# Two heads' values in seven block products among other groups; x's block differences and one gate group at other places

## The chip, the cores and the metric

The kernel runs on one core of a Trainium2 chip, in one launch. The metric is the device time of that launch in microseconds. TensorE multiplies matrices, VectorE and ScalarE work on elements, GpSimd builds constants, SyncE (SP) issues nearly all loads. In rows of the profile they are PE (its weight loads PEld), DVE, ACT, POOL and SP.

## The reference

One decoder block on x of 256 tokens and 2048 columns, in float32:

```
h = rmsnorm(x)
q, k, v, g, gk, gb, gc, xc, ma, mb = split(h @ w_in)           # 16,400 columns
log_g = log_sigmoid(gk @ w_gk_up + b) / 16                     # 4 heads, key width 256, value width 512
o = rmsnorm(gated linear attention of q, k, v, log_g)          # in chunks of 64, per head
y_a = o * silu(g);  y_b = gb * conv3(gc * xc)                  # causal, depthwise
x = x + (sigmoid(ma) * y_a + sigmoid(mb) * y_b) @ w_out
out = rmsnorm(x + (silu(h2 @ w_gate) * (h2 @ w_up)) @ w_down)  # h2 = rmsnorm(x), 5632 wide
```

## The kernel before

Every matrix is streamed once from HBM in *pieces* of 128 x 1024 numbers (0.5 MB): four blocks of 128 rows of a 256-column group (k and q), or two of a 512-column group (all else). A piece is split on the chip: ScalarE casts it to `hi` (`high`, L238), VectorE subtracts to get `lo` (`low`, L243), and `mm3` (L347 to L349) makes each product out of three matmuls, so that float32 precision is kept. The buffers are 5 raw pieces, 6 `hi` and 5 `lo`. `stream_list` gives the order of all pieces; `take` keeps loads, casts and subtractions up to LOOK = 5 pieces ahead of TensorE. After each piece `used` counts a *tick*, and work registered with `later(delay, fn)` or `at(tick, fn)` is issued at its tick. The program is then scheduled per engine: an instruction that is ready in the scheduler's plan can pass an earlier one that isn't, except those under `pin`.

A 512-column group normally takes 8 pieces (`eights`): 2 blocks of rows x 2 halves of the tokens x 3 matmuls of 512 columns, 12 per piece. A *pair* of groups can be done with seven block products in place of eight (`sevens`): 28 steps of 6 matmuls. In each of four quarters q a step `11` uses a block of the first group, `t1`, `t3`, `t2` and `t4` use sums of blocks that VectorE forms first (`sum_of`, L259 and L265, from loads `y` and `x`), and at the end eight steps `21` and `22` use plain blocks again. `sevens` needs five PSUM banks and block differences of the tokens' side (`xsums`, formed by `x_blocks` at the ticks of X_AT, four quarters; `sum_blocks` makes four subtractions, a cast and a low half). Steps stand between plain pieces of other groups (`mixed`), since a step needs as much from VectorE as a plain piece or more.

The stages: `mm_first` does k0, q0, v0 together (16 pieces, ticks 0 to 16) while x, its norm, the decay tables and GpSimd's differences are made. Then for heads 1 to 3: k, q and v, each plain (`mm_cols`, `mm_tok`); `scale_rows` scales k and q, `decayed` multiplies them into the decay tables, `scores` makes the scores, `values` splits v into `vh` and `vl`, `attend` multiplies (9 matmuls, `o_ps`), `head_norm` scales with the head's norm. Then the gates, in the order of GATES: g0 plain, and four pairs gc/xc in seven products with plain ma, gb, mb and g groups between, and gb3, mb3. At the third piece of g0 the heads' memory (`gla`, `gpool`) is given back, and the pools of the gates take its place, among them the one for `y` and `x`. A gate's result is merged (`merge`, `transpose_block`) while the next pair runs. Then come w_out, the feed-forward stage (its own pairs fg/fu among down pieces), and the last norm.

PSUM: banks b0 to b4 are for groups of five, b5, ax0 and ax1 are `lent` in turn to plain groups and transposes.

Of the kernel before, what the change touches and what calls it, by code (L numbers as in the profile page):

```python
# [8 lines left out]
F32 = mybir.dt.float32  # L9
# [11 lines left out]
H = 4  # L21
# [22 lines left out]
def plan():  # L44
# [61 lines left out]

def mixed(pair, eights, early=False):

    if pair is None:
        return eights  # L110
    sevens = seven_list(pair)
    sums = ("t1", "t3", "t2", "t4")
    gaps = [0] * len(sevens)
    rest = len(eights)
    while rest > 0:
        for some in (sums + ("11",) if early else sums, ("21", "22")):
            for n, (_, e) in enumerate(sevens):
                if e[0] in some and rest > 0:
                    gaps[n] += 1
                    rest -= 1  # L120
    out, put = [], 0
    for e, n in zip(sevens, gaps):
        out += [e] + eights[put:put + n]
        put += n
    return out


def gates_list():
    return [e for pair, keys in GATES
            for e in mixed(pair, [(key, k) for key in keys for k in range(0, KC, 2)], keys[0] == "gb2")]  # L130

# [45 lines left out]
def stream_list():  # L177

    pieces = [(p[0], p[3]) for p in piece_list()]
    out = [e for e in pieces if e[0][0] in "kqv"] + gates_list() + [e for e in pieces if e[0] == "wo0"]  # L180
    return out + hidden_list() + down_list()
# [3 lines left out]
def block_kernel(ctx, tc, x, xt, cols_in, gkw_in, gku_in, gnw, conv_w, finw, w_in, w_out, w_gu, w_dn, out):  # L185
# [25 lines left out]

    lent = ["b5", "ax0", "ax1"]


# [180 lines left out]

    count["sevens"] = 0

    def sevens(name, pool, a, s, second, done):

        r = 2 * count["sevens"]
        count["sevens"] += 1
        pa, pb, pc, pd, pe = (bank([P, 512], f"{name}_{i}", f"b{(r + i) % 5}") for i in range(5))
        v2, v3 = (pool.tile([P, 512], F32, tag=n, name=n) for n in ("v2", "v3"))
        u = {}
        for _ in range(28):
            piece, (what, q) = yield
            first, last = q == 0, q == 3
            if what == "11":  # L410
                quad(pa, lambda j: a(0, 4 * q + j), piece, first, last)
                if last:
                    nc.scalar.copy(v2, pa)
            elif what == "t1":
                quad(pb, lambda j: s(0, q, j), piece, first, last)
            elif what == "t3":
                quad(pd, lambda j: s(2, q, j), piece, first, last)
            elif what == "t2":
                quad(pc, lambda j: s(1, q, j), piece, first, last)
                if last:  # L420
                    u[1] = second(1)
                    nc.vector.tensor_tensor(out=v2, in0=pc, in1=v2, op=ALU.subtract)
                    nc.vector.tensor_tensor(out=v3, in0=pd, in1=v2, op=ALU.add)
# [12 lines left out]
        done(0, pa, u[0])  # L436
# [344 lines left out]
    at(25, tables_across)  # L781
    v_first = mm_first(gk_chunks, scale_rows)

# [3 lines left out]
    def x_blocks(q):  # L787
        pair = gpool.tile([P, NM, T], F32, tag="bc", name="xraw")
        raw, work = pair[:, 0:4, :], pair[:, 4:8, :].rearrange("p s (j c) -> p s j c", c=P)
        cs = slice(4 * q, 4 * q + 4)  # L790
# [3 lines left out]
    for q in range(4):  # L794
        at(X_AT[q], lambda q=q: x_blocks(q))


# [8 lines left out]
    def scores(i):  # L806

        ps = aux([P, 3, P], "sc_ps")
        ms = (2 * i, 2 * i + 1)
# [15 lines left out]

    o = [omain.tile([P, NT, DV], F32, tag=f"m{i}", name="o") for i in range(H)]
    sso = const.tile([P, NT, H], F32, name="sso")
    ro = const.tile([P, NT, H], F32, name="ro")

    def attend(i, vh, vl):  # L830
        sh, sl = sc.pop(i)
        ps = [aux([P, DV], "o_ps") for t in range(NT)]
        mm3(ps[0], sh[:, 0, :], sl[:, 0, :], vh[:, 0, :], vl[:, 0, :], True, True)
        mm3(ps[1], sh[:, 2, :], sl[:, 2, :], vh[:, 0, :], vl[:, 0, :], True, False)
        mm3(ps[1], sh[:, 1, :], sl[:, 1, :], vh[:, 1, :], vl[:, 1, :], False, True)
        for t in range(NT):
            nc.scalar.copy(o[i][:, t, :], ps[t])
            square_sum(o[i][:, t, :], sso[:, t, i:i + 1])

# [6 lines left out]
    split_v = {}  # L846
    for i in range(H):
        if i:
            for key, ps in [(key, mm_cols([key], xh, xl)[0]) for key in (f"k{i}", f"q{i}")]:
                scale_rows(key, ps)  # L850
        now = count["tick"]
        at(max(now + 1, 27 + i), lambda i=i: decayed(i, scaled_rows.pop(f"k{i}"), scaled_rows.pop(f"q{i}")))
        at(max(now + 3, 29 + i), lambda i=i: scores(i))
        vps = mm_tok(f"v{i}", KC, 512, xa) if i else v_first

        def values(i=i, vps=vps):
            vh = gpool.tile([P, NT, DV], F32R, tag="vh", name="vh")
            vl = gpool.tile([P, NT, DV], F32R, tag="vl", name="vl")
            for t in range(NT):
                nc.scalar.activation(vh[:, t, :], vps[t], AF.Copy, scale=r1[:, t:t + 1])  # L860
                nc.vector.scalar_tensor_tensor(out=vl[:, t, :], in0=vps[t], scalar=r1[:, t:t + 1],
                                               in1=vh[:, t, :].bitcast(F32), op0=ALU.mult, op1=ALU.subtract)
            split_v[i] = (vh, vl)

        if i:
            values()
        else:

            at(18, values)
        tick_of = max(count["tick"] + 1, 31)  # L870
        at(tick_of, lambda i=i: attend(i, *split_v.pop(i)))
        at(tick_of + 1, lambda i=i: head_norm(i))

# [93 lines left out]

    def begin_gate(key):
# [5 lines left out]
    xy = None  # L974
    steps = run(gates_list(), begin_gate)
    for n in steps:
        if n == 2:

# [155 lines left out]
    for _ in run(order, hidden):  # L1134
        pass
    count["gap"] = 1
    finb = sT.tile([P, D], F32, tag="sh", name="finb")
    nc.scalar.dma_start(finb, finw.to_broadcast([P, D]))
# [43 lines left out]
CONV_AT = 12  # L1182
X_AT = (50, 54, 58, 62)
H_AT = (2, 4, 6, 8)
# [56 lines left out]
```

## Time and profile before

| | |
|---|---|
| median of 3 runs | 1504.65 us (1503.75 to 1506.16) |
| the profiled execution | 1504.81 us, its span 1503.1 us |
| granted clock of TensorE, mean | 0.999 |
| matmuls | 7064 |
| read from HBM | 351.03 MB |

All numbers of a trace are those of the one profiled execution, and its times count from the start of the span. A timeline's row has start, duration, engine, line, operation, result <- operands, and in brackets the idle time before it with what ended it. Rows of TensorE overlap: a matmul of 512 columns shows 0.39 us, so the distance between starts tells the pace, not the duration. `lo`, `hi`, `y`, `x` and `o_ps` are the names in the program; all gc/xc matmuls carry the first name, `gc`.

### The profile page before, as it was taken

What the parts mean: (1) busy time and instruction counts of PE and PEld (TensorE: products, weight loads), DVE (VectorE), ACT (ScalarE), POOL (GpSimd) and SP (SyncE); (2) the same over time, 40 slices, a digit from 0 to 9 for tenths busy, and PEclk for the clock granted to TensorE, in tenths of its full rate; (3) what the DMA queues carried; (4) which work ended last, traced back from release to release, by engine and by line L of the source; (5) the groups of instructions that cost most, each with busy time, mean ns of one, the idle gap of its engine ahead of it and who ended that gap; (6) DMA issues with size and microseconds to landing.
All of it is one profiled execution on the core that took longest, in us unless ns stands there. A gap on an engine that the chain in (4) does not pass through costs nothing.

```text
span 1503.1 us, 19370 instructions
## 1 busy us (share of the span) xinstructions
PE 1489.7 (99%) x7064; PEld 1244.8 (83%) x7064; DVE 1277.8 (85%) x1283; ACT 864.1 (57%) x977; POOL 38.0 (3%) x60
## 2 busy tenths in 40 slices
PE   9999999999999999999999999999999999999997
PEld 8989988888887888888888888888888788888887
DVE  6785868979979878966689999999999999999975
ACT  7773546655655655654566755655565556565553
POOL 0030000000000000000000000000000000000000
PEclk9999999999999999999999999999999999999999
DMA  9656557876876878787677777776877788787782
GB/s 349 201 172 174 177 166 251 288 225 234 285 259 232 297 237 257 249 258 215 209 221 219 238 253 251 250 253 218 275 242 239 259 255 277 242 264 234 231 297 90
DMA packets 100128, 358.58 MB, mean 239 GB/s; under 512 B 11492, under 2 KB 11620, under 8 KB 99904
## 3 DMA queue, kind: packets, MB, share of 16 engines
q1 hardware_dynamic: 96656, 346.73, 70.8%
q0 software_dynamic: 2800, 8.89, 2.2%
q10 hardware_dynamic: 576, 1.72, 0.3%
q8 instruction: 55, 0.90, 0.2%
q14 instruction: 41, 0.34, 0.1%
HBM read 351.03 MB, written 2.10 MB: 235 GB/s over the span
## 4 chain that ended last, share of the span: by engine, by line
PE 53%; DVE 1%; issue 0%; ACT 0%; DVEq 0%; ACTq 0%
PE fg L347 8%; PE fg L349 8%; PE fg L348 8%; PE dn L347 5%; PE dn L349 5%; PE dn L348 5%; PE wo L347 2%; PE wo L348 2%; PE wo L349 2%; PE fu L349 1%; PE fu L347 1%; PE fu L348 1%; PE trb L595 1%; PE mb L349 0%; PE mb L348 0%
## 5 line engine op out<-in xcount | busy, mean ns | idle before, releaser
L243 DVE TENSOR_TENSOR lo<-raw,hi 128x1024 fp32r<-128x1024 f32 (+1 forms) x506 | 612.0, 1217 | 110.9 <-ACT hi L238 27.9
L238 ACT CAST hi<-raw 128x1024 fp32r<-128x1024 f32 (+1 forms) x506 | 523.9, 1047 | 269.9 <-PE gb L349 27.7
L238 ACT CAST hi<-x 128x1024 fp32r<-128x1024 f32 x144 | 151.7, 1053 | 267.4 <-DVE x L265 207.1
L243 DVE TENSOR_TENSOR lo<-x,hi 128x1024 fp32r<-128x1024 f32 x144 | 176.1, 1223 | 37.5 <-ACT hi L238 26.6
L347 PE MATMUL dn<-lo,acth 128*128 128x512 f32 (+1 forms) x368 | 140.7, 382 | 1.7 <-DVE h L1098 0.9
L349 PE MATMUL dn<-hi,acth 128*128 128x512 f32 (+1 forms) x368 | 139.9, 380 | 0.0
L348 PE MATMUL dn<-hi,actl 128*128 128x512 f32 (+1 forms) x368 | 139.9, 380 | 0.0
L265 DVE TENSOR_TENSOR x<-x,raw 128x1024 f32<-128x1024 f32 x96 | 117.0, 1218 | 12.0 <-DMA raw<-in_w_in_dram 7.7
L347 PE MATMUL fg<-lo,hh 128*128 128x512 f32 x288 | 112.4, 390 | 0.0
L349 PE MATMUL fg<-hi,hh 128*128 128x512 f32 x288 | 112.2, 390 | 0.0
L348 PE MATMUL fg<-hi,hl 128*128 128x512 f32 x288 | 112.2, 389 | 0.0
L347 PE MATMUL fg<-lo,sh 128*128 128x512 f32 x256 | 101.0, 395 | 0.0
L348 PE MATMUL fg<-hi,sl 128*128 128x512 f32 x256 | 99.9, 390 | 0.0
L349 PE MATMUL fg<-hi,sh 128*128 128x512 f32 x256 | 99.8, 390 | 0.0
L347 PEld LDWEIGHTS dn<-lo,acth 128*128 128x128 f32 x368 | 69.2, 188 | 15.8 <-DVE h L1098 1.8
L349 PEld LDWEIGHTS dn<-hi,acth 128*128 128x128 f32 x368 | 69.2, 188 | 13.3
L348 PEld LDWEIGHTS dn<-hi,actl 128*128 128x128 f32 x368 | 69.2, 188 | 12.9
L347 PEld LDWEIGHTS fg<-lo,hh 128*128 128x128 f32 x288 | 54.1, 188 | 11.8 <-DVE lo L243 0.5
L349 PEld LDWEIGHTS fg<-hi,hh 128*128 128x128 f32 x288 | 54.1, 188 | 11.3
L348 PEld LDWEIGHTS fg<-hi,hl 128*128 128x128 f32 x288 | 54.1, 188 | 11.0
L243 DVE TENSOR_TENSOR lo<-y,hi 128x1024 fp32r<-128x1024 f32 x48 | 58.5, 1218 | 4.8 <-ACT hi L238 2.1
L259 DVE TENSOR_TENSOR raw<-y,x 128x1024 f32<-128x1024 f32 x48 | 58.5, 1219 | 4.2 <-DMA y<-in_w_in_dram 3.3
(247 smaller groups left out, 3070.1 us busy)
## 6 DMA issues: line engine op xcount, KB each, us to landing
raw<-in_w_in_dram SPq DMA_DIRECT2D x254, 512.0 KB, 4.5
raw<-in_w_gu_dram SPq DMA_DIRECT2D x176, 512.0 KB, 4.4
raw<-in_w_dn_dram SPq DMA_DIRECT2D x88, 512.0 KB, 4.5
x<-in_w_gu_dram SPq DMA_DIRECT2D x32, 512.0 KB, 4.8
y<-in_w_gu_dram SPq DMA_DIRECT2D x32, 512.0 KB, 3.9
raw<-in_w_out_dram SPq DMA_DIRECT2D x32, 512.0 KB, 4.3
y<-in_w_in_dram SPq DMA_DIRECT2D x16, 512.0 KB, 4.4
x<-in_w_in_dram SPq DMA_DIRECT2D x16, 512.0 KB, 4.8
```

Of the source, the lines that this page charges most:

```text
L238: nc.scalar.copy(hi[:, ks, :], raw[:, ks, :])
L243: nc.vector.tensor_tensor(out=lo[:, ks, :], in0=raw[:, ks, :], in1=hi[:, ks, :].bitcast(F32), op=ALU.subtract)
L259: nc.vector.tensor_tensor(out=raw, in0=y, in1=held["x"], op=ALU.add)
L265: nc.vector.tensor_tensor(out=x, in0=x, in1=other, op=ALU.add)
L347: nc.tensor.matmul(ps, lhsT=sh, rhs=ml, start=first, stop=False, skip_group_check=onto)
L348: nc.tensor.matmul(ps, lhsT=sl, rhs=mh, start=False, stop=False, skip_group_check=onto)
L349: nc.tensor.matmul(ps, lhsT=sh, rhs=mh, start=False, stop=last, skip_group_check=onto)
L595: nc.tensor.transpose(out=ps[:, j, :], in_=src[:, j * P:(j + 1) * P], identity=ident)
```

## The change

Heads 2 and 3 no longer multiply v2 and v3 as two plain groups. They become the pair ("v2", "v3") of `sevens`. `heads_list` gives the new order: k1, q1 and half of v1 as before; then the pair's 28 steps, dealt among the rest of v1, k2, q2, k3, q3 and seven pieces of g0 (27 plain pieces); then four pieces of ma0, the last of g0, four of ma0. The heads' memory is given back after the fourth piece of ma0. The heads run in the same loop (`run`) as the gates now: `mm_cols` becomes `cols_group`, `values` of head 1 is registered at the end of its group, and `pair_values` splits heads 2 and 3 straight from the pair's banks. In GATES ma0 is gone, and g1, ma1, mb1, gb2 and others move one pair forward; the last pair has three plain groups beside it.

`x_blocks` moves from ticks 50, 54, 58 and 62 to 5, 8, 12 and 17, with its work in tiles of `omain`. Smaller edits: one buffer in place of two for `kr` and `qr` (head 1's scaling moves to tick 28), `attend` is issued per half of the tokens on lent banks, and squares are written in place.

```diff
 GATES = (
-    (None, ("g0",)),
-    (("gc0", "xc0"), ("ma0", "gb0", "mb0")),
-    (("gc1", "xc1"), ("g1", "ma1", "gb1")),
-    (("gc2", "xc2"), ("mb1", "g2", "ma2")),
-    (("gc3", "xc3"), ("gb2", "mb2", "g3", "ma3")),
+    (("gc0", "xc0"), ("g1", "gb0", "mb0")),
+    (("gc1", "xc1"), ("ma1", "gb1", "mb1")),
+    (("gc2", "xc2"), ("g2", "ma2", "gb2")),
+    (("gc3", "xc3"), ("mb2", "g3", "ma3")),
     (None, ("gb3", "mb3")),
...
+    def deal(some, most):
+        nonlocal rest
+        for n, (_, e) in enumerate(sevens):
+            if e[0] in some and most > 0 and rest > 0:
+                gaps[n] += 1
+                rest -= 1
+                most -= 1
+    if late is not None:
+        deal(("21", "22"), late)
+        while rest > 0:
+            deal(sums + ("11",), rest)
...
+def heads_list():
+    step = {"k": 4, "q": 4, "v": 2, "g": 2, "m": 2}
+    plain = [(key, k) for key in ("k1", "q1", "v1", "k2", "q2", "k3", "q3", "g0") for k in range(0, KC, step[key[0]])]
+    n = plain.index(("v1", 8))
+    gate = [("ma0", k) for k in range(0, KC, 2)]
+    return plain[:n] + mixed(("v2", "v3"), plain[n:-1], 4) + gate[:4] + plain[-1:] + gate[4:]
...
-                    u[1] = second(1)
+                    u[1] = pc if tags else second(1)
...
-        u[0] = second(0)
+        u[0] = pb if tags else second(0)
...
-        pair = gpool.tile([P, NM, T], F32, tag="bc", name="xraw")
+        raw, work = (omain.tile([P, 4, 2, P], F32, tag=tag, name=tag) for tag in ("m0", "m1"))
...
+    def pair_values(t, two, three):
+        if t == 1:
+            place_values(2)
+            both = gpool.tile([P, 2, NT, DV], F32R, tag="bc", name="both")
+            split_v[3] = [both[:, n] for n in range(2)]
+        for i, src in ((2, two), (3, three)):
+            split_value(i, t, src)
+        if t == 0:
+            for i in (2, 3):
+                later(i - 1, lambda i=i: attend(i, 0))
+                later(i - 1, lambda i=i: attend(i, 1, "b1"))
+                later(i, lambda i=i: head_norm(i))
...
+    def rows_done(key, ps):
+        i = int(key[1])
+        if i > 1:
+            scale_rows(key, ps)
+        else:
+            at(28, lambda: scale_rows(key, ps))
+        if key[0] == "q":
+            now = count["tick"]
+            at(max(now + 1, 28 + i), lambda: decayed(i, scaled_rows.pop(f"k{i}"), scaled_rows.pop(f"q{i}")))
+            at(max(now + 4, 31 + i), lambda: scores(i))
...
+    def begin_head(key):
+        if isinstance(key, tuple):
+            return sevens(key[0], held["pool"], xa, sums(xsums), None, pair_values, ("b4", "b0", "b2", "b1", "b3"))
+        if key[0] == "v":
+            return eights(key, xa, lambda ps: values(int(key[1]), ps))
+        tags = {"k1": ("b0", "b1"), "q1": ("b2", "b3")}.get(key)
+        return cols_group(key, xh, xl, rows_done, tags)
...
-        return eights(key, xa, gate(key), *([("b3", "b4")] if key == "g0" else []))
-    steps = run(gates_list(), begin_gate)
-    for n in steps:
-        if n == 2:
+        return eights(key, xa, gate(key), *([("b2", "b3")] if key == "ma0" else []))
+    order = heads_list()
+    for n in run(order + gates_list(), begin):
+        if n == order.index(("ma0", 6)):
             gla.close()
...
-X_AT = (50, 54, 58, 62)
+X_AT = (5, 8, 12, 17)
```

## Rows read from the trace of the kernel before

**Rows 1.** The page's part 1: busy time, share of the span, instructions.

```profile
PE 1489.7 (99%) x7064; PEld 1244.8 (83%) x7064; DVE 1277.8 (85%) x1283; ACT 864.1 (57%) x977; POOL 38.0 (3%) x60
```

**Rows 2.** Timeline of TensorE: start us, us, engine, line, operation, operands.

```profile
160.26 0.28 PE L347 MATMUL k<-xl,hi 128*128 128x256 f32 x1
...
168.90 0.28 PE L347 MATMUL q<-xl,hi 128*128 128x256 f32 x1
...
208.31 0.39 PE L347 MATMUL g<-lo,xh 128*128 128x512 f32 x1
...
227.35 0.39 PE L347 MATMUL gc<-lo,xh 128*128 128x512 f32 x1
```

**Rows 3.** Waits of TensorE: who waits for whom, total us, times, longest.

```profile
PE trb L595 <- DVE sb L908: 0.9, 1, 0.9
...
PE g L347 <- DVE lo L243: 0.7, 1, 0.7
...
PE gc L347 <- DVE lo L243: 0.5, 1, 0.5
```

**Rows 4.** Stretch, length; busy PE, PEld, DVE, ACT, POOL; clock; DMA share; GB/s.

```profile
92.00:225.00 133.00, 133.00 (x793) 118.87 (x792) 89.92 (x114) 66.71 (x90) 2.81 (x6) 1.00 0.57 175
...
350.00:390.00 40.00, 39.47 (x178) 32.04 (x177) 38.98 (x36) 21.27 (x24) 1.84 (x3) 1.00 0.63 213
...
700.00:1400.00 700.00, 698.68 (x3131) 575.45 (x3130) 642.24 (x615) 406.90 (x447) 2.23 (x3) 1.00 0.75 243
...
18.00:57.00 39.00, 39.00 (x262) 36.07 (x261) 26.40 (x40) 28.47 (x49) 0.32 (x1) 1.00 0.91 302
...
57.00:70.00 13.00, 13.00 (x109) 12.91 (x109) 8.92 (x12) 12.94 (x15) 0.00 (x0) 1.00 0.57 165
```

**Rows 5.** Timeline of VectorE and TensorE: low halves and their first matmuls.

```profile
77.23 1.20 DVE L243 TENSOR_TENSOR lo<-raw,hi 128x1024 fp32r<-128x1024 f32 x1
...
83.30 0.39 PE L347 MATMUL v<-lo,xh 128*128 128x512 f32 x1
...
188.40 1.23 DVE L243 TENSOR_TENSOR lo<-raw,hi 128x1024 fp32r<-128x1024 f32 x1 [0.43 <-issue]
...
200.84 0.39 PE L347 MATMUL v<-lo,xh 128*128 128x512 f32 x1
...
239.10 1.23 DVE L243 TENSOR_TENSOR lo<-x,hi 128x1024 fp32r<-128x1024 f32 x1
...
241.00 0.39 PE L347 MATMUL gc<-lo,xh 128*128 128x512 f32 x1
```

**Rows 6.** VectorE by line, 230 to 660: xcount | busy, mean ns | idle before.

```profile
L265 DVE TENSOR_TENSOR x<-x,raw 128x1024 f32<-128x1024 f32 x31 | 37.8, 1219 | 7.9 <-DMA raw<-in_w_in_dram 7.7
...
L259 DVE TENSOR_TENSOR raw<-y,x 128x1024 f32<-128x1024 f32 x15 | 18.3, 1220 | 3.4 <-DMA y<-in_w_in_dram 3.3
```

**Rows 7.** VectorE by line, 91 to 225.

```profile
L462 DVE TENSOR_TENSOR xraw<-xraw 128x256 f32<-128x256 f32 x16 | 6.1, 420 | 0.2
...
L861 DVE SCALAR_TENSOR_TENSOR vl<-v,r,vh 128x512 fp32r<-128x512 f32 x6 | 4.5, 748 | 4.7 <-ACT vh L860 4.6
...
L823 DVE TENSOR_TENSOR scl<-scr,sch 128x384 fp32r<-128x384 f32 x4 | 2.2, 560 | 3.6 <-ACT sch L821 3.6
...
L802 DVE TENSOR_TENSOR ek<-ek,kr 128x512 f32<-128x512 f32 x3 | 2.1, 688 | 0.1
...
L802 DVE TENSOR_TENSOR exk<-exk,kr 128x256 f32<-128x256 f32 x3 | 1.2, 414 | 0.0
...
L570 DVE RECIPROCAL ro<-ro 128x2 f32<-128x2 f32 x4 | 0.7, 166 | 5.2 <-ACT ro L569 5.2
```

**Rows 8.** ScalarE by line, 92 to 204.

```profile
L238 ACT CAST hi<-raw 128x1024 fp32r<-128x1024 f32 x38 | 39.7, 1051 | 44.7 <-PE v L349 20.0 <-PE q L349 11.0 <-PE k L349 10.1
```

**Rows 9.** SyncE, 195 to 230: a wait, and the timeline's row of y's load.

```profile
SPq L232 <- PE o_ps L349: 8.3, 1, 8.3
...
212.08 0.33 SPq L232 DMA_DIRECT2D y<-in_w_in_dram  x1
```

More of the change, by code (lines that the diff above doesn't have):

```diff
@@ L104, in seven_list, with mixed @@
     return [(pair, e) for e in out + list(twos)]
-def mixed(pair, eights, early=False):
+def mixed(pair, eights, late=None):
     if pair is None:
@@ L114, in mixed @@
     rest = len(eights)
-    while rest > 0:
[L116 to L120, printed above, removed]
+    def deal(some, most):
[9 more added lines that the diff above has]
+            deal(sums + ("11",), rest)
+    while rest > 0:
+        for some in (sums, ("21", "22")):
+            deal(some, rest)
     out, put = [], 0
@@ L179, in stream_list @@
     pieces = [(p[0], p[3]) for p in piece_list()]
-    out = [e for e in pieces if e[0][0] in "kqv"] + gates_list() + [e for e in pieces if e[0] == "wo0"]
+    out = [e for e in pieces if e[0] in ("k0", "q0", "v0")] + heads_list() + gates_list()
+    out += [e for e in pieces if e[0] == "wo0"]
     return out + hidden_list() + down_list()
@@ L394, in quad, with sevens @@
             mm3(ps, ah, al, hi[:, j, :], lo[:, j, :], first and j == 0, last and j == n - 1, onto)
[L396 to L405, printed above, removed]
+    count["sevens"] = 2
+    def sevens(name, pool, a, s, second, done, tags=None):
+        if tags is None:
+            r = 2 * count["sevens"]
+            count["sevens"] += 1
+        pa, pb, pc, pd, pe = (bank([P, 512], f"{name}_{i}", tags[i] if tags else f"b{(r + i) % 5}") for i in range(5))
+        v2 = pool.tile([P, 512], F32, tag="v2", name="v2")
         u = {}
@@ L806, in scores @@
     def scores(i):
[L808 removed]
+        ps = lend([P, 3, P], "sc_ps")
         ms = (2 * i, 2 * i + 1)
@@ L824, in scores, with attend @@
         sc[i] = (sh, sl)
-    o = [omain.tile([P, NT, DV], F32, tag=f"m{i}", name="o") for i in range(H)]
+    o = {}
     sso = const.tile([P, NT, H], F32, name="sso")
     ro = const.tile([P, NT, H], F32, name="ro")
[L830 to L838, printed above, removed]
+    def attend(i, t, tag=None):
+        sh, sl = sc[i]
+        vh, vl = split_v[i]
+        if i not in o:
+            o[i] = omain.tile([P, NT, DV], F32, tag=f"m{i}", name="o")
+        ps = bank([P, DV], "o_ps", tag) if tag else lend([P, DV], "o_ps")
+        if t == 0:
+            mm3(ps, sh[:, 0, :], sl[:, 0, :], vh[:, 0, :], vl[:, 0, :], True, True)
+        else:
+            mm3(ps, sh[:, 2, :], sl[:, 2, :], vh[:, 0, :], vl[:, 0, :], True, False)
+            mm3(ps, sh[:, 1, :], sl[:, 1, :], vh[:, 1, :], vl[:, 1, :], False, True)
+        nc.scalar.copy(o[i][:, t, :], ps)
+        square_sum(ps, sso[:, t, i:i + 1], ps)
     def head_norm(i):
@@ L846, in block_kernel @@
     split_v = {}
[L847 to L866, printed above, removed]
-        else:
[L869 to L872, printed above, removed]
@@ new lines, in split_value, with place_values, values @@
+    def split_value(i, t, src):
+        vh, vl = split_v[i]
+        nc.scalar.activation(vh[:, t, :], src, AF.Copy, scale=r1[:, t:t + 1])
+        nc.vector.scalar_tensor_tensor(out=vl[:, t, :], in0=src, scalar=r1[:, t:t + 1],
+                                       in1=vh[:, t, :].bitcast(F32), op0=ALU.mult, op1=ALU.subtract)
+    def place_values(i):
+        split_v[i] = [gpool.tile([P, NT, DV], F32R, tag=tag, name=tag) for tag in ("vh", "vl")]
+    def values(i, ps):
+        place_values(i)
+        for t in range(NT):
+            split_value(i, t, ps[t])
+        tick = max(count["tick"] + 1, 31)
+        for t in range(NT):
+            at(tick + 2 * t, lambda t=t: attend(i, t))
+        at(tick + 4, lambda: head_norm(i))
@@ new lines, in block_kernel, with __init__, tile @@
+    at(18, lambda: values(0, v_first))
+    class HeadsPool:
+        def __init__(self):
+            self.turn = 0
+        def tile(self, shape, dtype, tag, name, bufs=None):
+            if tag not in ("x", "v3"):
+                return gpool.tile(shape, dtype, tag=tag, name=name)
+            self.turn += 1
+            return omain.tile(shape, dtype, tag=f"m{2 + self.turn % 2}", name=name)
+    held["pool"] = HeadsPool()
+    def begin_head(key):
[5 more added lines that the diff above has]
+        return cols_group(key, xh, xl, rows_done, tags)
```

57 lines of the change are left out of this document (36 added, 21 removed).

## Prediction

> **What bounds the kernel now.** I read the page's engine shares first, then the list of waits on TensorE, then busy time by stretch, then single rows around the change. TensorE is busy 99% of the span, VectorE 85%, TensorE's weight loads 83% [rows 1]. A busy TensorE alone proves little, because its rows overlap; the start times prove it. From 208.31 to 227.35 us run 84 matmuls of 512 columns, so one starts every 19.04/84 = 0.2267 us. In the k and q groups 72 matmuls of 256 columns start from 160.26 to 168.90, one every 0.120 us [rows 2]. So a piece of 12 large matmuls takes 2.72 us, a k or q piece of 24 small ones 2.88, a step of a seven-product group (6 large ones) 1.36, a head's attention (9 large ones) 2.04. TensorE's longest waits in the gates' stage come to 0.9 + 0.7 + 0.5 us, all for VectorE [rows 3]; the granted clock is 1.00 in every stretch of rows 4. TensorE's own count of matmuls is the bound, as long as the others keep ahead of it.
>
> How far they keep ahead I call the lead: from the end of a piece's `lo` on VectorE to its first matmul. In the heads it is large: the `lo` of 188.40 ends at 189.62 and belongs to v3's last piece, whose matmuls start at 200.84, a lead of 11.2 us. In the gates the `lo` that starts at 239.10 ends at 240.33, and its matmul starts at 241.00, a lead of 0.7 [rows 5]. So the heads have room on VectorE (89.9 of 133.0 us busy from 92 to 225), the later stages hardly (38.98 of 40 from 350 to 390, 642.2 of 700 from 700 to 1400), and yet TensorE idles only 0.53 us and 1.32 us there [rows 4].
>
> **The change part by part.** Pieces are numbered in stream order: head 0 is 0 to 15; in the new order k1, q1 and half of v1 are 16 to 27, the mix of 28 steps with 27 plain pieces is 28 to 82, ma0 with g0's last piece 83 to 91, the first gc/xc step 92. Tick n comes right behind piece n - 1.
>
> *Products of v2 and v3.* Before: 2 groups x 8 pieces x 12 = 192 large matmuls. After: 28 steps x 6 = 168. 24 fewer at 0.2267 us: **-5.44 us**, all on the path, since TensorE starts one matmul right behind the other here. Attention, scores and the other groups keep their matmul counts, and ma0 and g0 only change place.
> The Trainium skill ("TensorE: Matmul & The Clock Gate", section "Wait — 56ns, not 53.3ns?") gives 215.7 ns from start to start for 512 columns at the full clock. By that figure the term would be an estimated 24 x 0.2157 = 5.18 us; the trace's 226.7 differs by 5%, and it decides.
>
> *What the other engines do for it.* 28 steps need 28 `lo`, where 16 pieces needed 16: 12 x 1.22. The sums t1 to t4 of four blocks: 16 x 1.22 [rows 6]. The five combinations at the end, 128x512 each: 5 x 0.69 [rows 7]. VectorE: 14.6 + 19.5 + 3.4 = 37.5 us more. ScalarE: 12 `hi` x 1.05 = 12.6 us [rows 8], where it idles 66.3 of 133 [rows 4]. DMA: 24 loads of 0.5 MB for 16, 4.2 MB more in about 128 us, 33 GB/s on top of 175; 243 are carried from 700 to 1400 [rows 4]. ScalarE and DMA: 0; a late load costs what a wait of VectorE costs, below.
>
> *x's block differences, now at ticks 5 to 17.* They leave the stretch from 92 to 225: 6.1 us of subtractions [rows 7] and per quarter a sum and a low half, 8 x 1.22 = 9.8, together 15.9 us of VectorE, 4.0 per quarter, and 4 ScalarE copies. Three quarters (11.9 us) go into 18 to 57, where VectorE idles 12.6 and ScalarE 10.5; the last into 57 to 70, where VectorE idles 4.1 but ScalarE nothing [rows 4]. That idle time is not all in the right place, so up to 3 us of VectorE's work may be pushed beyond 70. The lead there is smaller: the `lo` of 77.23 ends at 78.43, for the matmul at 83.30, 4.9 us [rows 5]. 4.9 - 3 is above zero: 0 taken. If that cover were gone, up to 3 us; a gain is excluded, since these differences ended no wait of TensorE before.
>
> *The mix itself.* VectorE from 92 to 225 becomes 89.9 - 15.9 + 37.5 + 1.7 (scaling of k1 and q1, four of 0.42, which moves from ticks 20 and 24 to 28) = 113.2 us, in 133.0 - 5.4 = 127.6: 89%, less than the 92% that the stretch from 700 to 1400 carries with the same kind of mix. There are two tight places. Ticks 26 to 30: five `lo` 6.1, two sums 2.4, two heads' decay products 2 x (2 x 0.69 + 2 x 0.41) = 4.4, k1's and q1's scaling 1.7, head 0's scores 1.0 make 15.6, and some 1.3 for rows that run long beside GpSimd, 16.9; TensorE has four plain pieces, one step and 12 small score matmuls (under 0.12 each), 13.6. In the last quarter of the sums (pieces 61 to 70): ten `lo` 12.2, four sums 4.9, scaling 0.8, decay products 2.2, scores 1.0, four combinations 2.8, two `vl` 1.5, 25.4; TensorE 6.8 + 5.8 + 8.2 + 1.4 = 22.2. Each is short by about 3.3; in between the two are even. A lead of about 5 before each covers it, and nothing but the lead does. Cost by the nearest rows: 1.32 us per 700 makes 0.24 in 128 us, 0.53 per 40 makes 1.7. I take **+1.0**, between them; the ends are 0 (TensorE has no idle time there to win) and the 8.4 of the first rival.
> The new waits: pieces 31 to 39 need the banks of k1 and q1, which tick 28 frees, 4 us and more ahead; behind a late one on TensorE stands all else. Head 1's attention comes right behind v1's last piece now and needs `vh` and `vl`, about 0.7 + 0.75 us on two engines; the order on an engine follows readiness, so the t3 step can go first. 0, at most 1.4.
>
> *ma0 beside the heads, and the way into the gates.* y's first load takes memory of the heads' pool. SP waited 8.3 us for head 3's attention, then for its norm, and issued the load at 212.08 [rows 9], 15.3 us before the matmul at 227.35 [rows 2]; that wait ate the lead of 11.2 down to 0.7. v3 ended at 200.84 + 2.72 = 203.56, so the release came 8.5 us behind it. Now two heads end together at piece 82: 8.5 + 2.0 for the second attention + 0.7 for the combination in front = 11.2 us behind its end. From there to piece 92 lie nine plain pieces and both attentions: 9 x 2.72 + 4.1 = 28.6, so 17.4 us remain, 2.1 more than now. 0: TensorE had no wait there to lose, and if the release is late it is the third rival.
>
> *Gates.* The pair gc3/xc3 has three plain groups beside it, where it had four, so a cover of eight pieces less where a merge falls; elsewhere g and ma only change places. The waits to win or lose are those of rows 3, 2.1 us in either direction. I take **+0.3**.
>
> Sum against the profiled execution: 1504.81 (span 1503.1, 1.7 around it) - 5.44 + 1.0 + 0.3 = 1500.67. That execution stands 0.16 above the median of the runs: **1500.5**.
>
> **Rivals.** *VectorE's waits (slower).* The mix leaves 127.6 - 113.2 = 14.4 us of idle time and a lead of 5: VectorE may wait 19.4 us in order before TensorE stops. Before, it waited 3.6 + 4.7 + 5.2 = 13.5 for ScalarE's casts, `vh` and norms [rows 7]. If these stay, the sums' loads add the 7.9 + 3.4 of the gates [rows 6] and the early differences their 3, it is 27.8: a stop of 8.4 us, 1504.81 - 5.44 + 8.4 + 0.3 - 0.16 = 1507.9. It turns slower than before from 24.5 us of waits on. For it: the lead of 0.7 in the gates. Against: the heads' waits come from being early, and a late VectorE doesn't wait for `vh`.
> The Trainium skill ("Perfetto Trace Analysis", "Identifying the Most-Contended Engine") judges TensorE by its weight loads and VectorE by occupancy; by that VectorE (85%) stands above the weight loads (83%), and work put on it makes the kernel slower. The trace speaks against it: TensorE idles 1.32 us of 700 while VectorE is 92% busy.
>
> *The gain is half spent (no change).* The two shortfalls of 3.3 find half the lead each: 3.3 lost in place of 1.0, 1502.8.
>
> *y's load comes later.* Head 3's norm d us later than counted: free up to d = 2.8 (2.1 + 0.7), then one for one; at d = 6, 1503.7.
>
> *The change does less than it says.* If banks or buffers hold each step, the products' gain is gone: 1504.6, as before; nothing in the rows asks for it.
>
> **How the numbers follow.** Forecast 0.62 (own range 1498.5 to 1501.9); VectorE's waits 0.13; half spent 0.12; y's load 0.08; does less 0.05. About 0.2% (3.0 us) is what a measurement tells from no change, so faster means under 1501.6: the forecast but for 0.03, and 0.07 out of the lower parts of "half spent" and "y's load": 0.66. Slower, over 1507.7: the first rival at full size, or the third with a larger d: 0.11. The rest, 0.23, is the same. The range: below, -5.44 with 1 us of the gates' 2.1 won and no loss in the mix, 1498.0; above, into the rivals to 1505.0, which leaves out less than 0.2.
>
> **What would show it.** Right: 168 matmuls for the two values 0.2267 us apart, TensorE's waits between 92 and 225 under 2 us in sum, VectorE 88 to 90% busy there, y's load 15 us or more ahead of its matmul, no new wait before 92. Wrong: a wait of TensorE of over 1 us near ticks 26 to 36 or in the last quarter of the sums, one at the first gc steps, or TensorE's waits in the gates grown by over 2 us.

## The result, and the profile after

The changed kernel takes 1508.18 us (median of 22 runs) where the kernel before takes 1505.32 (22 runs beside it): ratio 1.0020, interval 1.0012 to 1.0027. Forecast was 1500.5. The profiled execution took 1508.41 us, its span 1506.5, 3.4 more than before.

Part 1 of the page of the changed kernel answers to [rows 1]: 24 matmuls fewer, as counted, and VectorE 34.6 us busier.

```profile
PE 1487.1 (99%) x7040; PEld 1240.7 (82%) x7040; DVE 1312.4 (87%) x1316; ACT 874.6 (58%) x990; POOL 33.0 (2%) x60
```

The share of TensorE is 99% in both; the loss is not to be seen there. Busy time by stretch of the changed kernel (columns as in [rows 4], the first five rows answer to those; two more lie around a stop, and two are for the heads' start and the gates):

```profile
92.00:225.00 133.00, 132.16 (x784) 117.13 (x783) 111.44 (x128) 77.77 (x98) 0.94 (x3) 1.00 0.66 212
350.00:390.00 40.00, 40.00 (x178) 33.15 (x177) 39.30 (x37) 22.11 (x23) 5.01 (x9) 1.00 0.71 228
700.00:1400.00 700.00, 698.12 (x3127) 574.51 (x3126) 641.11 (x615) 406.83 (x447) 2.23 (x3) 1.00 0.74 243
18.00:57.00 39.00, 39.00 (x263) 36.10 (x262) 33.75 (x54) 30.89 (x51) 0.31 (x1) 1.00 0.87 309
57.00:70.00 13.00, 13.00 (x110) 13.00 (x110) 11.95 (x19) 12.84 (x15) 0.00 (x0) 1.00 0.69 222
...
85.00:88.50 3.50, 0.85 (x5) 0.38 (x4) 3.50 (x4) 2.30 (x2) 2.02 (x2) 1.00 0.00 0
88.50:93.00 4.50, 4.50 (x14) 3.56 (x13) 4.50 (x5) 4.50 (x5) 0.00 (x0) 0.62 0.78 236
...
70.00:92.00 22.00, 19.35 (x119) 17.24 (x118) 22.00 (x22) 11.54 (x10) 6.79 (x5) 0.93 0.34 105
...
350.00:660.00 310.00, 305.29 (x1351) 250.39 (x1350) 277.79 (x258) 174.43 (x182) 14.91 (x27) 1.00 0.76 255
```

The last two stretches in the kernel before:

```profile
70.00:92.00 22.00, 22.00 (x141) 20.03 (x140) 21.12 (x29) 13.91 (x12) 11.72 (x5) 1.00 0.48 144
...
350.00:660.00 310.00, 307.86 (x1366) 253.41 (x1365) 270.72 (x249) 175.78 (x183) 11.78 (x21) 1.00 0.77 254
```

TensorE idles 2.65 us of 70 to 92, a stretch of the heads in which VectorE and not TensorE is busy throughout, and behind that its granted clock is 0.62 in the mean from 88.5 to 93. TensorE's waits, first of 60 to 240, then of 350 to 660 (answering to [rows 3]):

```profile
PE v L375 <- DVE lo L271: 2.7, 1, 2.7
PE sc_ps L851 <- ACT o_ps L604: 0.8, 1, 0.8
...
PE ma L375 <- ACT ya L1015: 2.6, 2, 1.8
PE g L375 <- DVE lo L271: 1.2, 1, 1.2
PE gc L375 <- DVE lo L271: 0.5, 1, 0.5
PE trb L631 <- DVE sb L995: 0.3, 1, 0.3
```

In the kernel before, the list is empty from 60 to 240, and from 350 to 660 it has the three waits of [rows 3]. So the two in the heads are new, and so is the one for `ya`. Taking each start-to-start distance of TensorE's large and small matmuls above 0.2267 and 0.120 us as lost, the kernel before loses 15.4 us in all and the changed one 24.1: +8.7, less 5.44 for the 24 matmuls, makes +3.3, the difference of the spans but for 0.1. Of the 8.7, 5.7 lie between 50 and 150 us and 3.4 between 350 and 650; the rest is -0.4.

The stop in rows of the timeline of the changed kernel (GpSimd, VectorE, TensorE):

```profile
80.23 1.93 POOL L796 TENSOR_TENSOR exk<-bc 128x512 f32<-128x512 f32 x1 [27.91 <-DVE bc L769]
...
80.07 1.20 DVE L271 TENSOR_TENSOR lo<-raw,hi 128x1024 fp32r<-128x1024 f32 x1
81.18 1.53 DVE L786 TENSOR_TENSOR eq<-bc 128x512 f32<-128x512 f32 x1
82.63 1.26 DVE L787 COPY eq<-bc 128x512 f32<-128x512 f32 x1
...
86.03 3.21 DVE L271 TENSOR_TENSOR lo<-raw,hi 128x1024 fp32r<-128x1024 f32 x2
...
82.62 0.39 PE L375 MATMUL v<-lo,xh 128*128 128x512 f32 x1
...
85.12 0.39 PE L377 MATMUL v<-hi,xh 128*128 128x512 f32 x1
88.16 0.50 PE L375 MATMUL v<-lo,xh 128*128 128x512 f32 x1 [2.65 <-DVE lo L271]
...
89.32 0.63 PE L376 MATMUL v<-hi,xl 128*128 128x512 f32 x1
89.75 0.63 PE L377 MATMUL v<-hi,xh 128*128 128x512 f32 x1
```

The same operation in the kernel before:

```profile
78.35 0.68 DVE L750 TENSOR_TENSOR eq<-bc 128x512 f32<-128x512 f32 x1
```

VectorE makes its decay tables (`eq`, L786 and L787) while GpSimd makes the others (`exk`, `exq`, L796 to L800). L786 takes 1.53 us, where it takes 0.68 in the kernel before. So the low half of v1's third piece starts only at 86.03, 4.85 us behind the first of the four table operations, and TensorE waits. Behind the stop matmuls come to start 0.43 us apart, the pace of the lower clock level (1.2 GHz), until 92.3. By the distances that is 2.8 + 1.7 us, and the wait of 0.8 at the scores costs 1.0: together 5.5 of the 5.7.

### The profile page after: what moved, and what is told of

Its sections match the earlier page's. It is cut to its first block, busy times and chain, and to the rows that moved or that the text cites. A ratio compares the mean times of both kernels' runs of the same rounds, so it can differ in the third digit from the quotient of the medians.

```text
span 1506.5 us, 19393 instructions
## 1 busy us (share of the span) xinstructions
PE 1487.1 (99%) x7040; PEld 1240.7 (82%) x7040; DVE 1312.4 (87%) x1316; ACT 874.6 (58%) x990; POOL 33.0 (2%) x60
## 4 chain that ended last, share of the span: by engine, by line
PE 91%; DVE 5%; issue 1%; DMA 1%; ACT 1%; SPq 0%; DVEq 0%; ACTq 0%
PE fg L375 8%; PE fg L377 8%; PE fg L376 8%; PE dn L375 5%; PE dn L377 5%; PE dn L376 5%; PE gc L375 3%; PE gc L377 3%; PE gc L376 3%; PE wo L375 2%; PE mb L377 2%; PE mb L375 2%; PE mb L376 2%; DVE lo L271 2%; PE wo L376 2%; PE wo L377 2%
## 5 line engine op out<-in xcount | busy, mean ns | idle before, releaser
L271 DVE TENSOR_TENSOR lo<-raw,hi 128x1024 fp32r<-128x1024 f32 (+1 forms) x502 | 607.1, 1217 | 91.9 <-ACT hi L266 22.3
L266 ACT CAST hi<-x 128x1024 fp32r<-128x1024 f32 x156 | 164.2, 1053 | 287.4 <-DVE x L293 217.3
L271 DVE TENSOR_TENSOR lo<-x,hi 128x1024 fp32r<-128x1024 f32 x156 | 190.8, 1223 | 42.5 <-ACT hi L266 30.9
L375 PE MATMUL dn<-lo,acth 128*128 128x512 f32 (+1 forms) x368 | 140.7, 382 | 1.7 <-DVE h L1186 1.0
L293 DVE TENSOR_TENSOR x<-x,raw 128x1024 f32<-128x1024 f32 x104 | 126.8, 1219 | 12.6 <-DMA raw<-in_w_in_dram 7.8
L375 PE MATMUL fg<-lo,hh 128*128 128x512 f32 x288 | 112.4, 390 | 0.0
L375 PE MATMUL fg<-lo,sh 128*128 128x512 f32 x256 | 101.0, 395 | 0.0
L375 PEld LDWEIGHTS dn<-lo,acth 128*128 128x128 f32 x368 | 69.2, 188 | 15.8 <-DVE h L1186 1.8
L271 DVE TENSOR_TENSOR lo<-y,hi 128x1024 fp32r<-128x1024 f32 x52 | 63.4, 1219 | 4.1 <-PE g L375 1.4
L287 DVE TENSOR_TENSOR raw<-y,x 128x1024 f32<-128x1024 f32 x52 | 63.3, 1218 | 2.8 <-DMA y<-in_w_gu_dram 2.5
L293 DVE TENSOR_TENSOR x<-x,y 128x1024 f32<-128x1024 f32 x52 | 63.5, 1220 | 0.7
L375 PEld LDWEIGHTS fg<-lo,hh 128*128 128x128 f32 x288 | 54.1, 188 | 11.7 <-DVE lo L271 0.5
```

The source lines that it names most:

```text
L266: nc.scalar.copy(hi[:, ks, :], raw[:, ks, :])
L271: nc.vector.tensor_tensor(out=lo[:, ks, :], in0=raw[:, ks, :], in1=hi[:, ks, :].bitcast(F32), op=ALU.subtract)
L287: nc.vector.tensor_tensor(out=raw, in0=y, in1=held["x"], op=ALU.add)
L293: nc.vector.tensor_tensor(out=x, in0=x, in1=other, op=ALU.add)
L375: nc.tensor.matmul(ps, lhsT=sh, rhs=ml, start=first, stop=False, skip_group_check=onto)
```

## The experiments

All kernels are the changed kernel with an edit, unless it says the kernel before. Ratios are to the kernel before, run beside them (medians 1505.32 to 1505.83).

| kernel | median us | ratio (interval) |
|---|---|---|
| changed kernel | 1508.18 | 1.0020 (1.0012 to 1.0027) |
| e1 no x differences | 1507.77 | 1.0014 (1.0006 to 1.0023) |
| e2 before, x early | 1507.19 | 1.0007 (0.9998 to 1.0017) |
| e4 x split | 1507.58 | 1.0013 (1.0005 to 1.0022) |
| e7 no tables on GpSimd | 1504.26 | 0.9990 (0.9981 to 0.9999) |
| e8 banks | 1508.18 | 1.0021 (1.0010 to 1.0031) |
| e9 heads, three edits | 1511.00 | 1.0030 (1.0019 to 1.0042) |
| e10 taps | 1508.94 | 1.0023 (1.0014 to 1.0032) |
| e11 e9 and taps | 1509.53 | 1.0025 (1.0014 to 1.0035) |
| e12 tables on VectorE | 1503.56 | 0.9993 (0.9984 to 1.0002) |
| e13 gates' order | 1508.47 | 1.0025 (1.0015 to 1.0035) |
| e14 e12, x split, banks | 1504.49 | 0.9993 (0.9982 to 1.0004) |
| e15 e14 and gates' order | 1504.53 | 0.9997 (0.9988 to 1.0006) |
| e16 e14, attention later | 1503.25 | 0.9983 (0.9971 to 0.9996) |
| e17 before, tables on VectorE | 1503.85 | 0.9994 (0.9985 to 1.0003) |
| e18 e2, tables on VectorE | 1505.42 | 1.0001 (0.9992 to 1.0009) |
| e19 e14, attention at 36 | 1502.24 | 0.9978 (0.9968 to 0.9987) |
| e20 e19, convolution later | 1512.19 | 1.0040 (1.0025 to 1.0054) |

The theories at the start: (1) x's block differences, now early, push VectorE's work back until the tables are late; (2) the mix's 37.5 us of extra VectorE work is the loss; (3) the new order of the gates is.

**Is it the early differences? (e1, e2, e4)**

```
-    for q in range(4):
-        at(X_AT[q], lambda q=q: x_blocks(q))
+    for s in xsums:
+        nc.gpsimd.memset(s.bitcast(F32), 0.5)
```

> x's block differences are left out of the changed kernel (their sums are constants, so v2 and v3 are computed from other numbers); all else stays. Theory 1 (the early differences push VectorE until the decay tables run late and beside GpSimd's, and TensorE stops at 85 us and then gets a lower clock): the stop of 2.7 us and the clock of 0.62 behind it go, and the 1.0 us at 106 with them: 4.7 to 6 us below the changed kernel, about 1502.5 to 1503.5 on the scale of its 1508.2. Theory 2 (the 37.5 us of extra VectorE work in the mix itself): within 1 us of the changed kernel. Theory 3 (the new order of the gates): within 1 us as well, and the waits near 490 to 511 us stay.

```
-X_AT = (50, 54, 58, 62)
+X_AT = (5, 8, 12, 17)        # the kernel before, in tiles m0 and m1
```

> The kernel before, with nothing changed but the ticks of x's block differences (5, 8, 12, 17 in place of 50, 54, 58, 62, in the outputs' tiles m0 and m1). Theory 1: the same stop of TensorE near 85 us, 2 to 5 us longer than the kernel before, and a granted clock below 1.00 behind the stop. Theories 2 and 3: as before, within 1 us.

```
-X_AT = (5, 8, 12, 17)
+X_AT = (5, 8, 36, 45)        # the last two in the tile of "bc"
```

> The changed kernel, with x's first two quarters at ticks 5 and 8 as in it, but the last two at ticks 36 and 45, inside the mix, ahead of the steps that read them. Theory 1: the stop at 85 us and the low clock go, 4.5 to 6 us below the changed kernel, which is 2 to 3 us below the kernel before: 1502 to 1503.5. Theory 2 (VectorE's load in the mix costs the time): 7.9 us more of VectorE's work inside the mix make it slower than the changed kernel, by up to 3 us.

Theory 1 gave the right place and the wrong price. The stop at 85 went in e1 and e4, and another came 14 us later. Waits of TensorE in e1, 60 to 240:

```profile
PE o_ps L375 <- ACT sch L859: 2.7, 1, 2.7
PE o_ps L375 <- ACT scr L857: 0.2, 1, 0.2
```

Head 0's attention, due at 98.9, waits for its scores until 101.96, and the clock from 102 to 106 is 0.61. e2 has no stop at 85 but waits of 0.5 us at the scores and 0.7 at the attention (at 93 and 103); its 1.6 us can't be told from nothing.

**Do GpSimd and VectorE hold each other up? (e7)**

```
-        nc.gpsimd.tensor_tensor(out=exk[:, :, 0:C], ...)     # and four more on exk, exq
+        nc.gpsimd.memset(exk, -1.0)
+        nc.gpsimd.memset(exq, -1.0)
```

> The changed kernel without GpSimd's five operations on the decay tables (exk and exq are filled with a constant early, so that heads 0 to 3 decay wrongly); VectorE's work stays. If VectorE's table operations are late because they run beside GpSimd's: they take 0.68 and 0.42 us again in place of 1.53 and 1.26, lo(26) ends 2 to 2.5 us sooner, and the stop at 85 us shrinks under 0.8 us, with the clock at 1.00: 3 to 5 us below the changed kernel. If the backlog alone makes it (7.9 us of x's last two quarters): the stop stays above 1.5 us and the time within 1.5 us of the changed kernel's.

VectorE, then TensorE's waits (60 to 240), in e7:

```profile
80.89 0.69 DVE L786 TENSOR_TENSOR eq<-bc 128x512 f32<-128x512 f32 x1
...
82.76 2.36 DVE L271 TENSOR_TENSOR lo<-raw,hi 128x1024 fp32r<-128x1024 f32 x2
...
PE sc_ps L848 <- ACT o_ps L604: 1.9, 1, 1.9
```

The first branch held: 3.9 us below the changed kernel, intervals apart, and L786 back at 0.69. The four table operations take 1.87 us in place of 4.85, and the stop at 85 is gone although x's differences are still early. It was the only one of the first four that moved the time. One stop is left in it, at 101.1, 1.9 us for the bank of head 0's attention.

**Banks, attention, taps (e8 to e11)**

```
+                pc = one(2) if pc is None else pc            # b2 and b3 are taken from t2 and t4 on
-        ps = lend([P, 3, P], "sc_ps")
+        ps = bank([P, 3, P], "sc_ps", "b3") if i == 1 else lend([P, 3, P], "sc_ps")
-            at(tick + 2 * t, lambda t=t: attend(i, t))
+            at(tick + 2 * t, lambda t=t: attend(i, t, "b2" if t == 0 else None))
```

> The changed kernel, with more banks for heads 0 and 1: while v1's group holds two of the three lent banks, one bank (ax1) takes both heads' scores and attention halves in turn. Here scores(1) uses b3 and attention halves (0,0) and (1,0) use b2, which the mix takes only from its t2 and t4 on. Theory 4 (the single bank holds TensorE): the 1.0 us at 106 goes, 0.4 to 1.5 us below the changed kernel's 1508.2; the stop at 85 us stays. Theory 1 alone (late tables): no change.

e9 adds e4's edit and head 0's attention at tick 33:

> The three edits to the heads together: x's last two quarters at ticks 36 and 45, the extra banks, and head 0's attention (both halves) at tick 33 in place of 31 and 33. Theory 5 (three limits in a row, each hidden by the one in front: late tables, head 0's scores behind VectorE's queue, one bank): no stop of over 0.5 us from 85 to 115, clock 1.00 there, 5 to 6 us below the changed kernel, 1502 to 1503.5. If VectorE's load as such is the limit, the stop moves on to a later piece and the time stays within 1.5 us of the changed kernel's.

```
-        nc.gpsimd.dma_start(taps, ...)      # ahead of the copies of u
+        nc.gpsimd.dma_start(taps, ...)      # behind them
```

> The changed kernel with the load of the convolution's taps (one DMA of some 0.8 MB) issued behind the copies of u in place of ahead of them, so that it moves from 380 and 485 us to about 352, 461 and 565. Theory 3 (that burst makes a weight block late, ScalarE waits for it with the Silu of g2 behind, and ma2 waits for g2's banks): the wait of ma for ya near 497 (1.9 us in the changed kernel) falls under 0.5, the excess from 450 to 550 from 4.7 to about 2 us, and the time is 2 to 3 us below the changed kernel. If it is ScalarE's order alone: no change within 1 us.

> The heads' three edits and the taps' move together. If theories 5 and 3 both hold and add: 7 to 9 us below the changed kernel, 1499.5 to 1501.5, faster than the kernel before by 4 to 6 us, as the sum of the prediction had it. If they don't add, within 1.5 us of the heads' edits alone.

None of the four made the kernel faster. In e9 and e11 my edit made a stop of its own: with another turn of the lent banks, k2 got the one that held head 0's attention (`PE k L375 <- ACT o_ps L610`, 4.1 us). e10 told more than it was made for. It leaves the heads' instructions on TensorE, VectorE and ScalarE as they are, in the same order, and yet its profile looks quite different there. Timeline of e10: GpSimd, VectorE, ScalarE, TensorE.

```profile
80.63 11.82 POOL L796 TENSOR_TENSOR exk<-bc 128x512 f32<-128x512 f32 x1 [27.92 <-DVE bc L769]
92.43 1.03 POOL L798 TENSOR_TENSOR exk<-bc 128x512 f32<-128x512 f32 x1
...
81.58 0.68 DVE L786 TENSOR_TENSOR eq<-bc 128x512 f32<-128x512 f32 x1
...
90.87 0.68 DVE L840 TENSOR_TENSOR ek<-ek,kr 128x512 f32<-128x512 f32 x1
97.16 0.42 DVE L840 TENSOR_TENSOR exq<-exq,qr 128x256 f32<-128x256 f32 x1 [5.61 <-ACT exq L803]
...
94.50 1.06 ACT L802 ACTIVATE exk<-exk 128x1024 f32<-128x1024 f32 x1 [4.91 <-POOL exk L797]
...
98.07 1.03 PE L853 MATMUL sc_ps<-exq,exk 128*128 128x128 f32 x4 [4.48 <-ACT hi L266]
```

Here VectorE keeps its pace and GpSimd's first operation takes 11.8 us: it ends some 0.9 us after VectorE comes to rest at 91.55. Its neighbour takes 1.03 with VectorE at rest. `exk` is late, VectorE stands 5.6 us behind it in its queue, and the scores stop TensorE for 4.5. (The wait is put down to a `hi` of ScalarE; VectorE's last operation on `exk`, which these matmuls read, ended at 97.92.) So the same code has two outcomes, one engine or the other held up, and either costs a stop. e8 and e13 show 11.8 us too, e1 9.0, e4 and e9 8.4. The kernel before had it as well:

```profile
77.40 6.08 POOL L760 TENSOR_TENSOR exk<-bc 128x512 f32<-128x512 f32 x1 [25.84 <-DVE bc L733]
```

The Trainium skill ("SBUF — State Buffer", section "Who interferes with whom") says that a VectorE instruction with two inputs in SBUF and a GpSimd instruction that reads SBUF exclude each other, the first to issue keeping the shared read interface for its whole instruction. The rows agree that one blocks the other; they add that GpSimd's stayed blocked through a dozen VectorE instructions that followed each other without a gap.

**The tables on VectorE (e12), and the gates' order (e13)**

```
-        nc.gpsimd.tensor_tensor(out=exk[:, :, 0:C], in0=last(0), in1=ch(0), op=ALU.subtract)   # and 4 more
+        nc.vector.tensor_tensor(out=exk[:, :, 0:C], in0=last(0), in1=ch(0), op=ALU.subtract)   # and 4 more
```

> The changed kernel with one edit: GpSimd's five operations on the decay tables (exk, exq) run on VectorE. Theory 6 (the two engines hold each other up: in the profiles GpSimd's first of them takes 1.9 us when VectorE's neighbours take twice their time, and 8 to 12 us when VectorE's keep their time; either way the scores or a weight block are late): no VectorE row beside them is lengthened, exk is ready by 88 us, and the time falls although VectorE gets some 3.2 us more work: the stop near 85 becomes 1.5 to 2.5 us (3.2 us more against a lead of 1.0 to 1.4 in the run without GpSimd's five), the 4.5 us at the scores don't come, 1 to 4 us below the changed kernel. If VectorE's own load in the stretch is the cause: 2 to 4 us above the changed kernel.

This is 4.6 us below the changed kernel, with intervals apart, although VectorE, already full from 70 to 92, has 3.2 us more to do. Stretch and wait of e12:

```profile
70.00:92.00 22.00, 22.00 (x138) 19.92 (x137) 22.00 (x28) 13.94 (x13) 0.00 (x0) 1.00 0.41 124
```

```profile
PE sc_ps L851 <- DVE ek L840: 1.8, 1, 1.8
```

This is the main cause, shown: five operations on the wrong engine for this order. What is left is the backlog itself, 1.8 us at head 0's scores, without a fall of the clock. How the 4.6 us divide is less sure. The profiled execution of e12 is the fastest of its runs (1501.16); by the distances it loses 3.6 us less than the changed kernel between 50 and 150, and 3.1 less between 350 and 650, where the two kernels are the same code.

```
-    (("gc1", "xc1"), ("ma1", "gb1", "mb1")),
-    (("gc2", "xc2"), ("g2", "ma2", "gb2")),
+    (("gc1", "xc1"), ("ma1", "gb1", "g2")),
+    (("gc2", "xc2"), ("mb1", "ma2", "gb2")),
```

> The changed kernel with mb1 and g2 exchanged in the gates' list: pair 1 gets ma1, gb1, g2 and pair 2 mb1, ma2, gb2. Theory 7 (g2's end falls just behind the convolution, whose five VectorE operations make the loads bunch; ScalarE waits for one of them with the Silu behind it, and ma2 waits for g2's banks): the wait of ma for ya near 497 goes, a wait of the next group for mb1's sigmoid of under 1 us takes its place, the excess from 450 to 550 falls from 2 to 6 us to under 2, and the time by 1.5 to 3 us. If the wait belongs to the place and not to the Silu: no change within 1 us.

No change: the wait for `ya` went and 1.7 us of the transposes' wait for the merge (`PE trb L631 <- DVE sb L995`) took its place. That speaks for the place in the pair and against the Silu; no run parts the two further.

**What is behind it (e14 to e16)**

> x's last two quarters at ticks 36 and 45, the decay tables' five operations on VectorE, and heads 0 and 1 on more banks (scores(1) on b3, attention halves (0,0) and (1,0) on b2; k2 gets b5 and ax0 as in the changed kernel); head 0's attention at its old ticks. Theory 6 with the bank theory: no stop of over 0.6 us from 70 to 120, 5 to 7 us below the changed kernel, 1501 to 1503. If a further limit lies behind these: the stop moves on, and the time stays above 1505.

> The heads' edits of the run before and the exchange of mb1 and g2 together. If theories 6 and 7 hold and add: 7 to 10 us below the changed kernel, 1498.5 to 1501, below the kernel before by 4 to 7 us, as the prediction's sum had it. If they don't add: as the heads' edits alone within 1 us.

e14 took the stops at 85 to 107 away, and again another came: head 1's attention waits 1.7 us for `vl` at 110.5. In the kernel before, it stood behind a k piece of 2.9 us, here behind a step of the mix, 1.4. The time is e12's, and the gates' exchange adds nothing (e15).

```
-        tick = max(count["tick"] + 1, 31)
+        tick = max(count["tick"] + 1 + i, 31)
```

> The heads' edits of the run e14 (x's last two quarters later, decay tables on VectorE, more banks) and head 1's attention one tick later (35 and 37 in place of 34 and 36), behind k2's first piece of 2.9 us and not behind a half step of 1.4. If head 1's attention is merely too early for its values (1.7 us of waiting for vl in e14): the wait goes, 1 to 2.5 us below e14's 1504.5, so 1502 to 1503.5 and below the kernel before. If the stop moves on again: as e14 within 1 us.

The edit missed: on TensorE the first half of that attention stayed where it was, and so did the wait (2.1 us). That the median is 1.2 below e14's is therefore not its doing.

**Did the kernel before pay for it? (e17, e18)**

> The kernel before with one edit: GpSimd's five operations on the decay tables run on VectorE. Its profile has GpSimd's first one at 6.1 us too, but no stop of TensorE there. Theory 6 in its form for this kernel (the contention was there before, with nothing late behind it): within 1 us of the kernel before. If GpSimd's tables cost time in any order of the heads: 3 to 5 us below it, and then the change of heads is not what turned them into a stop.

> The kernel before with x's block differences early, as in e2 (which came out 1.6 us above the kernel before), and the decay tables on VectorE. If the early differences cost by way of the contention: back to the kernel before within 0.8 us. If they cost by VectorE's load alone: as e2 or above, since VectorE gets 3.2 us more.

Neither can be told from the kernel before. There the same contention is covered. And e12 and e17, the same edit on either kernel, come out alike: once the tables are out of the way the change loses nothing, but it gains nothing.

**The version that beats both (e19), and the gates once more (e20)**

```
-        tick = max(count["tick"] + 1, 31)
+        tick = max(count["tick"] + 1, 31) + 2 * i
-            at(tick + 2 * t, ...)
+            at(tick + (2 - i) * t, ...)
```

> As e16, but head 1's attention at ticks 36 and 37, so that on TensorE its first half stands behind k2's first piece (in e16 the order on TensorE had kept it behind the half step, and the wait of 2.1 us for vl stayed). If that wait is the last stop in the heads: none of over 0.5 us from 70 to 235, 1.5 to 3 us below e14 and e16, 1500.5 to 1502.5, and 3 to 5 us below the kernel before. If the time stays within 0.8 us of e16's 1503.25: the wait was covered by something else that ends as late.

The median is 1502.24, ratio 0.9978: 3.2 us below the kernel before, 5.9 below the changed one. Against e12 the gain is not clear of noise; the two intervals overlap. Busy time by stretch and waits (60 to 240, then 350 to 660) of e19:

```profile
70.00:92.00 22.00, 22.00 (x138) 19.87 (x137) 21.45 (x31) 15.33 (x14) 0.00 (x0) 1.00 0.38 107
92.00:225.00 133.00, 132.28 (x785) 117.28 (x784) 116.66 (x139) 77.96 (x102) 0.94 (x3) 1.00 0.65 204
...
350.00:660.00 310.00, 306.44 (x1356) 251.27 (x1355) 277.24 (x256) 173.20 (x182) 14.04 (x26) 1.00 0.78 259
```

```profile
PE k L375 <- DVE vl L905: 0.7, 1, 0.7
...
PE ma L375 <- ACT ya L1027: 2.4, 2, 2.0
```

A wait of 0.7 us is left of all stops in the heads (between 50 and 150 it loses 1.3 more than the kernel before by the distances), with VectorE at 116.7 of 133, more than in the changed kernel. Theory 2 falls with that.

```
-            later(CONV_AT + n, ...)
+            later((20 if i < 3 else CONV_AT) + n, ...)       # and merge_at in the same way
```

> As e19, and in the first three pairs of the gates the convolution's five VectorE operations (and the merge that follows) start 20 ticks behind the pair's end in place of 12, that is behind the end of the group that falls there (g2 in pair 2). Theory 8 (those five operations make VectorE's sums and so the loads late just as a group's banks are to be freed): the excess of TensorE from 350 to 650 falls from 4 to 7 us to under 3.5, 1 to 3 us below e19. If the place is late for another reason: no change within 0.8 us, or the stop moves to the merge's transposes.

It went the other way, by 10 us: three waits of 2.1 to 2.2 us for low halves, some 110 us apart (`PE gb L375 <- DVE lo L271: 2.1, 1, 2.1` is one), and a mean granted clock of 0.98 from 350 to 660, where e19 has 1.00. From 350 to 660 TensorE idles 2.1 us in the kernel before, 1.1 in e17 with the same gates, 4.7 in the changed one, 1.6 in e8, 1.9 in e12, 2.6 in e13, 3.2 in e10, 3.6 in e19 and 8.0 in e20. So the new order of the gates costs from nothing to 2.6 us of idle time, differently in kernels with the same gates; what decides it stays open.

## Why the prediction was wrong

By the distances, the -5.44 came as forecast, the heads lost 5.7 us where +1.0 stood, the gates 3.4 where +0.3 stood, and the rest gained 0.4.

*Products of v2 and v3: right.* 24 matmuls fewer, and the heads of e19 run at the old pace but for 1.3 us.

*VectorE's load, mix, last quarter of the sums: right in the main.* Counted were 113.2 us of 127.6 (89%); the changed kernel has 111.44 of 133 (84%), under the 88 to 90% that were to show it. From 120 to 225 TensorE is busy 105.00 of 105.00 us. The first rival, VectorE's waits adding up over the mix, did not happen; its time, 1507.9, came near by luck.

*The first tight place, "Ticks 26 to 30", failed.* The step was "each is short by about 3.3 ... A lead of about 5 before each covers it", with "some 1.3 for rows that run long beside GpSimd". Two things in it were wrong. One: it priced the contention as a lengthening of VectorE's rows only, at the 1.3 us of the kernel before; in the changed kernel's profile that is 3.8 (the table operations 4.85 against e7's 1.87, two low halves 3.21 against 2.36). And it never asked for GpSimd's own row: 6.1 us in the row of before shown above, 8.4 to 11.8 in e1, e4, e8 to e11 and e13. The other: it took the lead of `lo` for the lead of everything. The scores and the attentions have none of that lead; they come through tables, scaling, two casts and a copy in in-order queues. Since a step of the mix is half a piece and counts a tick too, ticks pass faster from 28 on, and head 0's attention is due at 98.9 in place of 102.3. Where +1.0 stood, the stop and the clock behind it cost 4.5 us in this profile; 4.6 us of the time come back where the contention is taken out (e12).

*x's block differences, "4.9 - 3 is above zero: 0 taken": the lead fell further than the bound of 3.* At v1's second piece it is 1.36 us (from 81.26 to 82.62), before it was 4.9; VectorE's 33.75 of 39 and 11.95 of 13 us from 18 to 70 show why. In the changed kernel's profile the contention then used up the rest. Taken alone (e1, e4) the early differences are worth under 1 us, because what they uncover costs as much.

*Attention, "0, at most 1.4":* 1.6 to 2.2 us in e8, e9, e11 and e14 to e16, which all have e8's banks. *Banks:* the 1.0 at 106 was not in the sum. v1 holds two of the three lent banks, so that scores and attentions of two heads pass through one; in e8 and e14, which have more banks, that wait is gone.

*Way into the gates: right.* Timeline of SyncE and VectorE in the changed kernel:

```profile
231.00 0.33 SPq L260 DMA_DIRECT2D y<-in_w_in_dram  x1
...
238.23 1.23 DVE L271 TENSOR_TENSOR lo<-y,hi 128x1024 fp32r<-128x1024 f32 x1 [0.37 <-PE g L375]
```

The load is 18.3 us ahead of its matmul at 249.29 (17.4 was forecast), and the third rival is out. *Gates, +0.3 with 2.1 either way:* +2.6 by idle time in this profile, 3.4 by distances, outside the 2.1; in e12, with the same gates, 0.3. Why stays open.

With the stops of the heads taken out (e19) the kernel is at 1502.24, against 1500.5 forecast; the gates' idle time there is 1.4 above before, that of the heads 0.7.

## What to carry to other kernels

Every consumer has its own lead, the time from its operand's end to its start: before a stage is made shorter, follow each chain that ends in it (scores, tables, banks), not the streamed operand's alone, and count in time, not in ticks, where the new ticks are shorter. An operation on GpSimd beside a VectorE that never rests is not free and has no fixed price; ask how long it takes in the profile against its time alone, and who waits for it. Where one stop goes and the time doesn't, look for the next stop behind it: here several stood in a row (85, 99, 106, 110), and moving one uncovered the next.

## What was not expected of the hardware

The same instructions in the same order came out in two ways: GpSimd's 128x512 subtraction at 1.93 us with VectorE's at 1.53 (0.68 alone), or at 11.82 with VectorE's unchanged (changed kernel and e10). Runs of the changed kernel spread from 1505.5 to 1512.6; that the two ways make this spread was not tested.

The granted clock fell behind a stop of 2.8 us in the changed kernel (0.62 in the mean from 88.5 to 93), one of 2.1 in e7 (0.64 from 103.4 to 107.5) and one of 2.0 in e14 (0.53 from 496 to 499.5). It stayed at 1.00 behind one of 1.9 in e12 (94 to 98) and one of 2.2 in e19 (495 to 499). Stops are by the distance of starts; their length alone does not tell these apart.
